# Order of the first transfers of a decoder trunk layer: the second block of x behind the first weights' loads, the stores of the first h behind the copies of its keys

## The chip, the cores and the metric

The kernel runs on one core of one Trainium2 chip. The metric is the device time of one execution in microseconds (us): the median of three runs is 3142.17 us (3137.32 to 3142.69). A core has TensorE (PE, with its weight loads shown apart as PEld), VectorE (DVE), ScalarE (ACT), GpSimd (POOL) and SyncE (SP). Nearly all transfers of this kernel are issued by SP, one after the other, and all of them are carried by the same set of 16 DMA engines.

## The reference, cut to what matters

One decoder layer on a sequence of 2048 tokens with 1024 features, all float32. The conditioning vector c gives shifts, scales and gates; the normed and modulated x goes through one input projection; two kinds of causal attention run on 8 heads each; then come an output projection with a gated residual, a gated MLP with a short convolution, and a last norm.

```python
mod = jax.nn.silu(c) @ w_ada[l] + b_ada[l]
shift_a, scale_a, gate_a, shift_m, scale_m, gate_m = [...]
h = rms_norm(x, g_attn[l]) * (1.0 + scale_a) + shift_a
proj = h @ w_in[l]
q_f, k_f, v_f, q_s, k_s, v_s, f_logit = jnp.split(proj, offsets, axis=-1)
...
o_fox = forgetting_attention(...); o_sb = stick_breaking_attention(...)
x = x + gate_a * (mix @ w_out[l])
h = rms_norm(x, g_mlp[l]) * (1.0 + scale_m) + shift_m
u = causal_depthwise_conv(h @ w_up[l], conv_w[l], conv_b[l])
x = x + gate_m * ((jax.nn.silu(u_gate) * u_val) @ w_down[l])
return rms_norm(x, g_final)
```

## The kernel before, in words

Tokens are worked in four blocks of 512 (`TB`), features in eight tiles of 128 (`kt`). A matrix product in float32 is made of three products of a high and a low part, so that each operand is split: `split` copies the rounded value with ACT (line 44) and subtracts it from the source with DVE or POOL (line 45).

The attention is worked in 32 units (kind, pair of heads, block), first the stick-breaking kind ("sb"). While one unit attends, the projections of the next one are worked in between (`interleave`). The order of the instructions on each engine's queue isn't the order of the program: a planner simulates the kernel's instructions and puts each on its engine's queue when it is ready in that simulation; earlier lines of the program go first among ready ones. The queues themselves are then worked in order, SP's too: a transfer whose operand isn't ready holds up all that stand behind it on SP.

The unit ("sb", 0, 0) stands alone at the start, and it also makes what the others need:

- `load_x` (line 173) brings a block of x as four tiles of 128 tokens. There are four buffers `xt`, so the second block can be loaded as soon as the transposes of the first have read it.
- `mod_cols(kt)` brings two pieces of `w_ada` (line 206; three buffers `ada`, one in use per `kt`) and multiplies them with silu(c): DVE takes five of eight parts (lines 209 and 211), ACT three (line 213) with POOL (line 215), then TensorE sums over the partitions (line 220), and DVE makes the column of shift and scale `mod_a` (lines 221, 222).
- `load` in `load_w` brings a tile of `w_in` (line 256; three buffers `wraw` for the query/key and the value columns together) and splits it. In `prepare` there is one query/key tile for each `kt`, and at the last `kt` also the eight tiles `raw_v` of the values.
- `modulate` norms x (lines 93 to 95 and 104), transposes it (line 112), applies shift and scale (line 117 with ACT for the first block, line 115 with DVE for the others) and splits it to `hp` (lines 44 and 45). There are ten buffers `hp`.
- `done` (line 364) stores each finished `hp` to DRAM (`hs`, line 366), where units of other heads fetch it (line 346), and accumulates the queries and, for the first block, the keys (line 281).
- `finish_proj` splits queries and keys, copies them with SP to the layout of the attention (Q: line 293, K: line 303), projects the values from `hp` (line 320) and stores the values of the next pair of heads (line 337).

The attention of a unit starts with logits (lines 378 and 379), which need Q and K; with line 410 ACT then takes sigmoids, with line 416 DVE scans them.

Of the kernel before, what the change touches and what calls it, by code (L numbers as in the profile page):

```python
# [1 line left out]

# [14 lines left out]
P = 128  # L17
S = 2048
D = 1024
KT = D // P  # L20
HD = 64
NH = 8
NPAIR = 8
TB = 512
# [9 lines left out]
def kernel(ctx: ExitStack, tc: tile.TileContext, x, c, w_ada, b_ada, g_attn, w_in, b_fgate,  # L34
                      g_out_fox, g_out_sb, w_out, g_mlp, w_up, conv_w, conv_b, w_down, g_final, out):
    nc = tc.nc
    x, out = x[0], out[0]
    w_ada, w_in, w_out, w_up, conv_w, w_down = w_ada[0], w_in[0], w_out[0], w_up[0], conv_w[0], w_down[0]

    def f(t):  # L40
        return t.bitcast(F32)
# [8 lines left out]
    hs = [[dram.tile([P, 2, TB], F32, name=f"hs{t}_{k}") for k in range(KT)] for t in range(NTB)]  # L50
# [107 lines left out]
    sb = open_pool("sb", side="right")  # L158
# [8 lines left out]
    pt = lambda: bank(psb, "pt", 3)  # L167
    pv = lambda: bank(psb, "pv", 1)

    def load_x(tb):  # L170
        xts = [px.tile([P, D], F32, name="xt", tag="xt", bufs=4) for _ in range(TB // P)]
        for i, xt in enumerate(xts):
            nc.sync.dma_start(xt, x[tb * TB + i * P:tb * TB + (i + 1) * P, :])
        return xts

    def h_tile():
# [26 lines left out]
    def mod_cols(kt):  # L203
        w = sm.tile([P, KT, 2, P], F32, name="ada", bufs=3)
        for i in range(2):
            nc.sync.dma_start(w[:, :, i], w_ada[:, i * D + kt * P:i * D + (kt + 1) * P].rearrange(
                "(k p) n -> p k n", p=P))
        t = sm.tile([P, 2, P], F32, name="adas", bufs=2)
        nc.vector.tensor_scalar_mul(t, w[:, 0], cs[:, 0:1])
        for k in range(1, 5):  # L210
            nc.vector.scalar_tensor_tensor(t, w[:, k], cs[:, k:k + 1], t, ALU.mult, ALU.add)
        for k in range(5, KT):
            nc.scalar.activation(w[:, k], w[:, k], AF.Copy, scale=cs[:, k:k + 1])
            if k > 5:
                nc.gpsimd.tensor_add(w[:, 5], w[:, 5], w[:, k])
        ts = [t, w[:, 5]]
        b = pv()
        for i in range(2):
            for n, t in enumerate(ts):
                nc.tensor.matmul(b[:, i:i + 1], t[:, i], ones[:, 0:1], start=n == 0, stop=n == len(ts) - 1)  # L220
        nc.vector.tensor_add(mod_a[:, 1, kt:kt + 1], b[:, 0:1], cols[:, R_BA + kt:R_BA + kt + 1])
        nc.vector.scalar_tensor_tensor(mod_a[:, 0, kt:kt + 1], b[:, 1:2], cols[:, R_GA + kt:R_GA + kt + 1],
                                       gba[:, kt:kt + 1], ALU.mult, ALU.add)
# [26 lines left out]
    def load_w(kind, p):  # L250
        base = (0 if kind == "fox" else 3 * 512) + p * P
        lo_engine = nc.vector if kind == "sb" else None

        def load(tag, kt, first, step):
            raw = sl_.tile([P, 2, P], F32, name=f"raw_{tag}", tag="wraw", bufs=3)
            nc.sync.dma_start(raw, w_in[kt * P:(kt + 1) * P, first:first + (step + 1) * P].rearrange(
                "p (a n) -> p a n", n=P)[:, 0:step + 1:step, :])
            n = 2 * P + (NH if tag == "v" else 0)
            w_ = sl_.tile([P, 2, n], F32R, name=f"w_{tag}", bufs=8)
            w = w_[:, :, 0:2 * P].rearrange("p s (a n) -> p s a n", n=P)  # L260
            split(w[:, 0], w[:, 1], raw, lo_engine)
            if tag == "v" and (kind, p) == ("sb", 0):
                split(w_[:, 0, 2 * P:], w_[:, 1, 2 * P:], wfr[:, kt], nc.vector)
            return w if tag == "qk" else w_

        def load_qk(kt):
            qk_.append(load("qk", kt, base, 4))

        def load_v():
            return [load("v", kt, base + 1024, 1) for kt in range(KT)] if p % 2 == 0 else None  # L270

        qk_ = []
        if (kind, p) == ("sb", 0):
            return [qk_, load_qk, load_v]
        for kt in range(KT):
            load_qk(kt)
        return [qk_, load_v()]
# [5 lines left out]
    def finish_proj(kind, p, tb, aq, w, hts, res, ak=None):  # L283
        Q = sb.tile([P, 2, 2, TB], F32R, name="Q", bufs=2)
        K = sb.tile([P, 2, TB], F32R, name="K", bufs=5)
        V = sb.tile([P, 4, 2, P], F32R, name="V", bufs=6)
        q2 = sl_.tile([P, 2, TB], F32R, name="q2", bufs=2)
        k2 = sl_.tile([P, 2, TB], F32R, name="q2", bufs=2)
        nc.scalar.activation(q2[:, 0], aq, AF.Copy, scale=-HD ** -0.5)
        nc.vector.scalar_tensor_tensor(q2[:, 1], aq, -HD ** -0.5, f(q2[:, 0]), ALU.mult, ALU.subtract)  # L290
        for h in range(2):
            for r in range(2):
                nc.sync.dma_start(f(Q[r * HD:(r + 1) * HD, h]), f(q2[h * HD:(h + 1) * HD]))
        if ak is None:
            ak = pj()
            for kt in range(KT):
                accumulate(ak, 1, w[0], hts[kt], kt)
                if kt % 2:
                    yield
        split(k2[:, 0], k2[:, 1], ak, nc.vector)  # L300
        for h in range(2):
            for r in range(2):
                nc.sync.dma_start(f(K[r * HD:(r + 1) * HD, h]), f(k2[h * HD:(h + 1) * HD, r]))
        yield
        spill = vs[kind][p // 2][tb]
        if p % 2:
            nc.sync.dma_start(f(V), spill)
        else:
            V1 = sb.tile([P, 4, 2, P], F32R, name="V", bufs=6)
            forget = (kind, p) == ("sb", 0)  # L310
            step, width = (1, 2 * P + NH) if forget else (2, 2 * P)
            if forget:
                zn = px.tile([P, 4, NH], F32, name="zn", bufs=1)
            for i in range(0, 4, step):
                av = pj()
                for t in range(step):
                    tok = slice((i + t) * P, (i + t + 1) * P)
                    for kt in range(KT):
                        for m, (a, bb) in enumerate(((0, 0), (0, 1), (1, 0))):
                            nc.tensor.matmul(av[:, t * width:(t + 1) * width], hts[kt][:, a, tok],  # L320
                                             w[1][kt][:, bb, 0:width],
                                             start=kt == 0 and m == 0, stop=kt == KT - 1 and m == 2)
                        if kt % 4 == 3:
                            yield
                if forget:
                    nc.vector.tensor_copy(zn[:, i], av[:, 2 * P:width])
                av = av[:, 0:step * 2 * P].rearrange("p (t e h d) -> p t e h d", t=step, e=2, h=2)
                for e, v in enumerate((V, V1)):
                    v = v[:, i:i + step]
                    split(v[:, :, :, 0:HD], v[:, :, :, HD:P], av[:, :, e], nc.vector)  # L330
            if forget:
                b = pt()
                nc.tensor.transpose(b[0:4 * NH, 0:P], zn.rearrange("p t n -> p (t n)"), ident)
                zt = px.tile([4 * NH, P], F32, name="zt", bufs=1)
                nc.scalar.activation(zt, b[0:4 * NH, 0:P], AF.Identity, bias=bf_c)
                nc.sync.dma_start(zs[tb], zt)
            nc.sync.dma_start(spill, f(V1))
        res.append((Q, K, V))
        yield
# [13 lines left out]
    def norm_proj(tb, xts, w, res):  # L353
        aq = pj()
        ak = qk() if tb == 0 else None
        def prepare(kt):
            mod_cols(kt)
            w[1](kt)
            if kt == KT - 1:
                w[1:] = [w[2]()]  # L360

        hts = []

        def done(kt, h):
            hts.append(h)
            nc.sync.dma_start(hs[tb][kt], f(h))
            accumulate(aq, 0, w[0], h, kt)
            if ak is not None:
                accumulate(ak, 1, w[0], h, kt)

        yield from modulate(px, pt, xts, mod_a, lambda kt: h_tile(), done, "a", nc.vector if tb == 0 else None, tb > 0,
                            f(sb.tile([P, 2, 2 * 2 * P], F32R, name="at", bufs=3)).rearrange("p a n -> p (a n)"),
                            prepare if tb == 0 else None)
        yield from finish_proj("sb", 0, tb, aq, w, hts, res, ak)

    def logits(cw, qcols, hl, Q, K):
        b = qk()
# [281 lines left out]
    for i, u in enumerate(units):  # L659
        kind, p, tb = u  # L660
# [13 lines left out]
        if kind == "fox":  # L674
            n = sum(2 * (2 + 2 * tb + j2 + 1) for j2 in range(2)) + 1
        else:
            n = sum(2 * (tb + 1 + 2 * tb + j2 + 1) for j2 in range(2)) + 1
        if i >= len(units) - 2:
            head_scale(i - len(units) + 2, pt(), sx)
        if nxt is None:  # L680
# [4 lines left out]
            loaded = [load_o(0, p) for p in range(3)]  # L685
# [37 lines left out]
    for u in range(NU):  # L723
# [3 lines left out]
        xts = []  # L727
# [293 lines left out]
```

## Time and profile before

| | |
|---|---|
| median of three runs | 3142.17 us (3137.32 to 3142.69) |
| the profiled execution | 3141.04 us, of which the span is 3139.3 us |
| TensorE matmuls | 2967.0 us busy, 95% of the span |
| TensorE weight loads | 2511.6 us, 80% |
| DVE / ACT / POOL | 2145.5 / 1691.0 / 1227.1 us |
| TensorE's granted clock, mean | 0.983 |
| first stretch, 0 to 80 us | PE busy 53.37 us, clock 0.89, DMA at 262 GB/s |

A row of the timeline gives start in us, length in us, engine, line, operation, what is written from what is read, the number of merged instructions, and in brackets the idle time of the engine before it with what ended it. SPq and ACTq are the issuing of transfers by SP and ACT: their length is the time of the issue and not that of the transfer. A row of a table by stages gives start and end, length, then for PE, PEld, DVE, ACT and POOL the busy time with the number of instructions, then the granted clock, the share of the DMA engines and the GB/s moved.

### The profile page before, as it was taken

The numbers are of one execution on the slowest core, as the hardware profiler recorded it, in microseconds if no ns is written. First come the engines' busy times: TensorE is split into PE (matmuls) and PEld (weight loads), VectorE is DVE, ScalarE is ACT, GpSimd is POOL, SyncE is SP. The second block draws the span as 40 slices with busy tenths as digits, with TensorE's granted clock in tenths as the row PEclk, the third lists the DMA queues.
The fourth block names the chain that finished last, engine by engine and source line by source line (L and its number), as shares of the span: only waits on it lengthen the run. The fifth ranks groups of instructions, "written<-read, shape, count | busy, mean of one in ns | idle before, by whom it ended". The sixth has DMA issues, their size and how long they took to land. (4 is left out here: it accounts for less than half of the span.)

```text
span 3139.3 us, 46425 instructions
## 1 busy us (share of the span) xinstructions
PE 2967.0 (95%) x15934; PEld 2511.6 (80%) x15934; DVE 2145.5 (68%) x3342; ACT 1691.0 (54%) x3161; POOL 1227.1 (39%) x1387
## 2 busy tenths in 40 slices
PE   6889998989989999999999999999899998999998
PEld 5778787877878889888877678888678887888887
DVE  6787888878875876556843587778987776354253
ACT  5666776666756676567744444444444444343332
POOL 1554455456553242242212344344444442322321
PEclk8999999999999999999999999999999999999999
DMA  9547542555336696585446632222222223554552
GB/s 267 177 140 255 168 136 69 182 185 155 123 108 221 214 314 211 158 313 162 164 158 222 212 97 86 86 83 83 82 82 89 85 81 130 190 199 161 189 199 90
DMA packets 292940, 496.51 MB, mean 158 GB/s; under 512 B 29448, under 2 KB 177664, under 8 KB 291680
## 3 DMA queue, kind: packets, MB, share of 16 engines
q1 hardware_dynamic: 281072, 480.92, 47.9%
q10 hardware_dynamic: 11632, 12.63, 1.1%
q8 instruction: 126, 2.06, 0.3%
q14 instruction: 110, 0.90, 0.1%
HBM read 352.61 MB, written 90.51 MB: 141 GB/s over the span
## 5 line engine op out<-in xcount | busy, mean ns | idle before, releaser
L810 PE MATMUL ps_o<-oa,wu 128*128 128x512 f32 x2088 | 503.5, 392 | 14.4 <-DVE oa L45 6.9
L810 PEld LDWEIGHTS ps_o<-oa,wu 128*128 128x128 f32 x2088 | 390.5, 188 | 105.5 <-DVE oa L45 10.7
L397 PE MATMUL ps_pv<-at,V 128*128 128x256 f32 x2304 | 410.9, 296 | 41.6 <-DVE at L393 24.8
L393 DVE TENSOR_TENSOR at<-ps_pt,at 128x512 fp32r<-128x512 f32 (+1 forms) x576 | 366.0, 653 | 102.8 <-ACT at L392 99.8
L281 PE MATMUL ps_pj<-hp,w_qk 128*128 128x512 f32 x1512 | 418.4, 406 | 11.1 <-ACT hp L44 3.1
L420 POOL TENSOR_TENSOR a<-a,r 128x512 f32<-128x512 f32 (+3 forms) x240 | 283.4, 1182 | 368.8 <-DVE r L416 112.3
L392 ACT ACTIVATE at<-ps_pt 128x512 fp32r<-128x512 f32 (+1 forms) x576 | 319.4, 577 | 179.8 <-PE ps_pt L388 147.3
L397 PEld LDWEIGHTS ps_pv<-at,V 128*128 128x128 f32 x2304 | 337.0, 192 | 84.6 <-DVE at L393 42.8
L281 PEld LDWEIGHTS ps_pj<-hp,w_qk 128*128 128x128 f32 x1512 | 275.7, 191 | 65.4 <-POOL hp L45 4.0
L45 DVE TENSOR_TENSOR wd<-wdraw,wd 128x1024 fp32r<-128x1024 f32 x88 | 112.4, 1277 | 261.4 <-ACT wd L44 261.4
L378 PE MATMUL ps_qk<-K,Q 128*128 128x512 f32 (+2 forms) x640 | 264.1, 414 | 11.3 <-DMA K<-q 5.8
L419 DVE TENSOR_TENSOR_SCAN r<-r 128x513 f32<-128x513 f32 x192 | 258.0, 1355 | 21.7 <-ACT r L410 14.5
L45 POOL TENSOR_TENSOR g<-graw,g 128x512 fp32r<-128x512 f32 x84 | 141.3, 1684 | 326.8 <-ACT g L44 326.8
L960 PE MATMUL ps_o<-wd,g 128*128 128x512 f32 x1040 | 250.8, 391 | 8.8 <-ACT g L44 8.8
L810 PE MATMUL ps_t<-ob,wu 128*128 128x512 f32 x984 | 243.2, 392 | 0.0
L320 PE MATMUL ps_pj<-w_v,hp 128*128 128x256 f32 (+1 forms) x1536 | 234.1, 291 | 4.8 <-DVE q L45 2.2
L379 PE MATMUL ps_qk<-K,Q 128*128 128x512 f32 (+2 forms) x640 | 238.1, 373 | 0.0
L960 PEld LDWEIGHTS ps_o<-wd,g 128*128 128x128 f32 x1040 | 196.2, 189 | 50.0 <-ACT g L44 9.2
L44 ACT ACTIVATE wu<-wuraw 128x512 fp32r<-128x512 f32 x214 | 133.2, 626 | 185.5 <-PE ps_o L810 111.5
L320 PEld LDWEIGHTS ps_pj<-w_v,hp 128*128 128x128 f32 x1536 | 211.8, 193 | 15.5 <-DVE q L45 3.1
L810 PEld LDWEIGHTS ps_t<-ob,wu 128*128 128x128 f32 x984 | 186.2, 189 | 39.4 <-DVE wu L45 0.3
L388 PE MATMUL ps_pt<-edge,a 128*128 128x128 f32 x1088 | 187.3, 281 | 27.6 <-POOL a L420 14.7
(217 smaller groups left out, 5743.3 us busy)
## 6 DMA issues: line engine op xcount, KB each, us to landing
hp<-hs SPq DMA_DIRECT2D x224, 512.0 KB
wuraw<-in_w_up_dram SPq DMA_DIRECT2D x84, 512.0 KB
wdraw<-in_w_down_dram SPq DMA_DIRECT2D x84, 512.0 KB
Q<-q SPq DMA_DIRECT2D x128, 256.0 KB
g<-u SPq DMA_DIRECT2D x42, 512.0 KB
graw<-g SPq DMA_DIRECT2D x84, 256.0 KB
hs<-hp SPq DMA_DIRECT2D x32, 512.0 KB
K<-q SPq DMA_DIRECT2D x128, 128.0 KB
```

Source lines behind the costliest of these rows:

```text
L45: (lo_engine or nc.gpsimd).tensor_sub(lo, src, f(hi))
L281: nc.tensor.matmul(acc, w[kt][:, a, n], h[:, bb], start=kt == 0 and i == 0, stop=kt == KT - 1 and i == 2)
L320: nc.tensor.matmul(av[:, t * width:(t + 1) * width], hts[kt][:, a, tok], w[1][kt][:, bb, 0:width], start=kt == 0 and m == 0, stop=kt == KT ...
L378: nc.tensor.matmul(b[:, :cw], Q[:, hl, 0, qcols], K[:, hl, :cw], start=True, stop=False)
L379: nc.tensor.matmul(b[:, :cw], Q[:, hl, 1, qcols], K[:, hl, :cw], start=False, stop=True)
L392: nc.scalar.activation(at[:, 0, lo:], b[:, lo:], AF.Copy)
L393: nc.vector.tensor_sub(at[:, 1, lo:], b[:, lo:], f(at[:, 0, lo:]))
L397: nc.tensor.matmul(o[:, 0:2 * P], V[kt // 4][:, kt % 4, hl, :], rhs, start=first and kk == 0 and w == 0, stop=last and kk == 1 and w == 1)
L419: nc.vector.tensor_tensor_scan(rev, rev, rev, 1.0, ALU.mult, ALU.bypass)
L420: (nc.vector if (ch + qi) % 4 == 0 else nc.gpsimd).tensor_mul(a[:, :need], a[:, :need], r[:, 1:need + 1])
L810: nc.tensor.matmul(b, w[:, p, j], o[:, q], start=first and i == 0, stop=last and i == 2, skip_group_check=True)
L960: nc.tensor.matmul(banks[t][n], g[:, a, t * P:(t + 1) * P], w[:, b, n * TB:(n + 1) * TB], start=k == 0 and i == 0, stop=k == NKD - 1 and i ...
```

## The change

Two groups of transfers of the first stretch get an earliest place on SP's queue. `tc.issue_after(ins)` makes every instruction of the block that runs on the engine of `ins` stand behind `ins` on that engine's queue. It gives an order of issue alone: nothing waits for the transfer of `ins` to have landed.

- The list `first_loads` collects the loads of `w_ada` (line 206) and the loads of `w_in` of ("sb", 0) (line 256). The block of x loaded first is loaded while the list is empty and stays as it is. The second block of x (and the later ones) is issued behind the last of them, the load of the eighth tile `raw_v`.
- The stores of the eight `hp` of the first block go from `done` to a place behind the last of the four copies of the first K (line 303). The stores of the later blocks stay in `done`.

The same tiles and the same bytes are moved as before.

```diff
+    first_loads, copied = [], []
+
+    def behind_first_loads():
+        return tc.issue_after(first_loads[-1].ins) if first_loads else nullcontext()
+
     def load_x(tb):
         xts = [px.tile([P, D], F32, name="xt", tag="xt", bufs=4) for _ in range(TB // P)]
-        for i, xt in enumerate(xts):
-            nc.sync.dma_start(xt, x[tb * TB + i * P:tb * TB + (i + 1) * P, :])
+        with behind_first_loads():
+            for i, xt in enumerate(xts):
+                nc.sync.dma_start(xt, x[tb * TB + i * P:tb * TB + (i + 1) * P, :])
         return xts
...
-            nc.sync.dma_start(w[:, :, i], w_ada[...])
+            first_loads.append(nc.sync.dma_start(
+                w[:, :, i], w_ada[...]))
...
+            if (kind, p) == ("sb", 0):
+                first_loads.append(loaded)
...
-                nc.sync.dma_start(f(K[r * HD:(r + 1) * HD, h]), f(k2[h * HD:(h + 1) * HD, r]))
+                copied[:] = [nc.sync.dma_start(f(K[r * HD:(r + 1) * HD, h]), f(k2[h * HD:(h + 1) * HD, r]))]
...
         def done(kt, h):
             hts.append(h)
-            nc.sync.dma_start(hs[tb][kt], f(h))
+            if tb:
+                nc.sync.dma_start(hs[tb][kt], f(h))
...
-        yield from finish_proj("sb", 0, tb, aq, w, hts, res, ak)
+        finish = finish_proj("sb", 0, tb, aq, w, hts, res, ak)
+        if tb == 0:
+            next(finish)
+            with tc.issue_after(copied[-1].ins):
+                for kt, h in enumerate(hts):
+                    nc.sync.dma_start(hs[tb][kt], f(h))
+        yield from finish
```

More of the change, by code (lines that the diff above doesn't have):

```diff
@@ L1 @@
-from contextlib import ExitStack
+from contextlib import ExitStack, nullcontext
 import concourse.bass as bass
@@ L205, in mod_cols @@
         for i in range(2):
-            nc.sync.dma_start(w[:, :, i], w_ada[:, i * D + kt * P:i * D + (kt + 1) * P].rearrange(
-                "(k p) n -> p k n", p=P))
+            first_loads.append(nc.sync.dma_start(
+                w[:, :, i], w_ada[:, i * D + kt * P:i * D + (kt + 1) * P].rearrange("(k p) n -> p k n", p=P)))
         t = sm.tile([P, 2, P], F32, name="adas", bufs=2)
@@ L255, in load @@
             raw = sl_.tile([P, 2, P], F32, name=f"raw_{tag}", tag="wraw", bufs=3)
-            nc.sync.dma_start(raw, w_in[kt * P:(kt + 1) * P, first:first + (step + 1) * P].rearrange(
+            loaded = nc.sync.dma_start(raw, w_in[kt * P:(kt + 1) * P, first:first + (step + 1) * P].rearrange(
                 "p (a n) -> p a n", n=P)[:, 0:step + 1:step, :])
+            if (kind, p) == ("sb", 0):
+                first_loads.append(loaded)
             n = 2 * P + (NH if tag == "v" else 0)
```

## The prediction, made before the result was known

> **What bounds the kernel now.** I read the page first (span, the row of slices, the sizes of the transfers), then tables by stages to see which stretch the change can reach, then the timelines of SP, DVE, ACT and PE over the first 80 us. The chain of waits that ended last doesn't reach back to the start, so the start has to be read from the timelines themselves.
>
> ```profile
> span 3139.3 us, 46425 instructions
> hs<-hp SPq DMA_DIRECT2D x32, 512.0 KB
> xt<-in_x_dram SPq DMA_DIRECT2D x16, 512.0 KB
> ```
>
> ```profile
> 14.60:50.60 36.00, 27.25 (x117) 20.97 (x118) 30.54 (x71) 21.91 (x50) 11.98 (x14) 0.86 1.16 325
> ...
> 60.00:70.00 10.00, 6.39 (x41) 5.48 (x39) 6.50 (x17) 4.59 (x12) 0.00 (x0) 0.95 0.90 210
> 70.00:80.00 10.00, 9.85 (x67) 9.74 (x68) 3.31 (x11) 3.01 (x14) 0.78 (x5) 0.83 0.15 34
> ...
> 80.00:200.00 120.00, 104.61 (x649) 90.61 (x649) 91.72 (x135) 78.07 (x172) 65.56 (x76) 0.94 0.48 164
> 200.00:800.00 600.00, 550.60 (x3484) 479.81 (x3483) 501.37 (x686) 403.94 (x893) 306.94 (x460) 0.98 0.53 165
> 800.00:1560.00 760.00, 730.08 (x4790) 650.58 (x4790) 528.00 (x1223) 504.11 (x980) 278.35 (x368) 0.99 0.62 200
> ```
>
> The reader is to see that from 14.6 to 50.6 us the DMA engines are full (share 1.16, 325 GB/s) and that DVE is close to full as well: 30.54 of 36 us. From 70 to 80 us the same engines are nearly empty (0.15, 34 GB/s), while PE is busy for 9.85 of 10 us. So bytes moved from the first stretch to the second lie beside other work. Which of DMA and DVE holds up the first stretch decides how much is won.
>
> SP's issues of the transfers in question:
>
> ```profile
> 1.20 1.78 SPq L173 DMA_DIRECT2D xt<-in_x_dram  x4
> ...
> 23.77 0.35 SPq L366 DMA_DIRECT2D hs<-hp  x1
> ...
> 29.24 0.42 SPq L366 DMA_DIRECT2D hs<-hp  x1
> ...
> 36.57 1.64 SPq L366 DMA_DIRECT2D hs<-hp  x1
> ...
> 40.15 0.38 SPq L366 DMA_DIRECT2D hs<-hp  x1
> 40.63 1.52 SPq L206 DMA_DIRECT2D ada<-in_w_ada_dram  x2
> 42.24 4.00 SPq L173 DMA_DIRECT2D xt<-in_x_dram  x3
> ...
> 48.24 0.88 SPq L256 DMA_DIRECT2D raw_v<-in_w_in_dram  x2
> ...
> 53.50 5.17 SPq L366 DMA_DIRECT2D hs<-hp  x2
> 59.43 0.84 SPq L256 DMA_DIRECT2D raw_v<-in_w_in_dram  x2
> 61.24 1.18 SPq L303 DMA_DIRECT2D K<-q  x2
> 62.52 3.18 SPq L293 DMA_DIRECT2D Q<-q  x4
> 65.80 2.30 SPq L303 DMA_DIRECT2D K<-q  x2
> 68.20 1.57 SPq L256 DMA_DIRECT2D raw_qk<-in_w_in_dram  x3
> ...
> 195.47 0.38 SPq L256 DMA_DIRECT2D raw_qk<-in_w_in_dram  x1
> ```
>
> Four stores stand ahead of the last pair of w_ada pieces, the second block of x is issued right behind that pair and ahead of five of the eight raw_v, and the last two raw_v leave 1.8 us before the first copy of K.
>
> **The change part by part.**
>
> **Stores of h.** Four of the eight stores stand ahead of the last w_ada pair. Four times 512 KB is 2.10 MB, at 325 GB/s 6.5 us of the DMA engines. That is the most that the pair can land earlier. What DVE can use of it is its own idle time after the first store; these are the rows in which it waited until it began the last `mod_cols`:
>
> ```profile
> 32.43 0.35 DVE L209 TENSOR_SCALAR adas<-ada,cs 128x256 f32<-128x256 f32 x1 [0.83 <-DMA ada<-in_w_ada_dram]
> 33.11 0.69 DVE L45 TENSOR_TENSOR hp<-hf_a,hp 128x512 fp32r<-128x512 f32 x1 [0.33 <-ACT hp L44]
> ...
> 38.75 0.16 DVE L221 TENSOR_TENSOR mod_a<-ps_pv,cols 128x1 f32<-128x1 f32 x1 [0.54 <-PE ps_pv L220]
> ...
> 47.78 0.16 DVE L221 TENSOR_TENSOR mod_a<-ps_pv,cols 128x1 f32<-128x1 f32 x1 [0.19 <-PE ps_pv L220]
> ...
> 49.63 0.69 DVE L45 TENSOR_TENSOR hp<-hf_a,hp 128x512 fp32r<-128x512 f32 x1 [1.49 <-ACT hp L44]
> 50.59 0.35 DVE L209 TENSOR_SCALAR adas<-ada,cs 128x256 f32<-128x256 f32 x1 [0.26 <-DMA ada<-in_w_ada_dram]
> ```
>
> Their sum is 0.83 + 0.33 + 0.54 + 0.19 + 1.49 + 0.26 = 3.6 us. DVE works in order, so its waits for ACT or PE go as well only if the next weights are there to be worked on; with the DMA relieved they are. I take 3.6 us, since DVE is the nearer limit; the bounds are nothing (other waits in the same places) and the 6.5 us of the bytes. On SP eight issues of some 0.4 us leave the first 60 us; SP is idle between issues there, so that counts for nothing by itself.
>
> Behind the copies of K the stores are 4.2 MB, 13 us at 325 GB/s. The cover is the stretch from 62 to 80 us, which moves 34 GB/s at its end. Cost: nothing. If the cover were gone, the ring of ten `hp` would show it: two buffers are free, so the third `hp` of the second block would wait for the first store, by at most the 13 us of all stores. Behind the stores on SP stand the three weight loads of 68.20, whose buffers are asked for again only at 195.47 us, so that nobody waits for them early.
>
> **Second block of x.** It moves from 42.24 us to behind the last raw_v. What leaves its old place, beside 2.10 MB, is its norm: squares on ACT and scalings on DVE that stand between h and the keys now.
>
> ```profile
> 60.01 1.42 DVE L104 TENSOR_SCALAR xt<-xt,ss_a 128x1024 f32<-128x1024 f32 x2
> 61.34 0.68 DVE L290 SCALAR_TENSOR_TENSOR q<-ps_pj,q 128x512 fp32r<-128x512 f32 x1
> 61.95 1.41 DVE L104 TENSOR_SCALAR xt<-xt,ss_a 128x1024 f32<-128x1024 f32 x2
> 63.27 0.68 DVE L45 TENSOR_TENSOR q<-ps_qk,q 128x512 fp32r<-128x512 f32 x1
> ```
>
> ```profile
> 55.94 1.04 ACT L93 ACTIVATE at<-xt 128x1024 f32<-128x1024 f32 x1
> ...
> 56.98 0.62 ACT L44 ACTIVATE hp<-hf_a 128x512 fp32r<-128x512 f32 x1
> ...
> 67.72 1.28 ACT L410 ACT_TABLE_LOAD   x1
> ```
>
> ```profile
> 70.15 0.39 PE L378 MATMUL ps_qk<-K,Q 128*128 128x256 f32 x1 [3.59 <-DMA K<-q]
> ...
> 78.70 0.60 PE L112 MATMUL ps_pt<-edge,xt 128*128 128x128 f32 x4
> ```
>
> The last `hp` stands 1.04 us behind a square: I take 0.9 us of that. The low parts of q and k stand between scalings of 2.83 us; the low part of k can start 2.0 us earlier (the one pair ahead of it costs 1.41, and the first pair pushes q by about 0.6 of its 1.42, as q's high part comes late anyway). K is landed at 70.15 us and PE has waited 3.59 us for it, so a K that comes earlier moves PE at once. I take 2.0 us. Bounds: 0 (if SP's issues of the Q copies, 3.18 us, are the limit anyway) and the 2.83 us of all four scalings. The raw_v are no longer behind x, so the splits of the value weights move forward into DVE's and ACT's waits, at no cost.
>
> The second block is needed at 78.70 us by the transposes. Even with raw_v at their old 59.43 us, the bytes of x take 6.5 us, then four squares of 1.04 us and four scalings of 0.71 follow: 59.4 + 0.8 + 6.5 + 4.2 + 0.7 is about 72 us. It fits by 6 us. If it slipped behind the sigmoids of the first attention, two table loads of 1.28 us would come on top: 2.6 us, the bound of this term upwards.
>
> The unknown of this part is where x stands against K. The trace doesn't show the new place. If raw_v leaves well ahead of K's copies, x is carried before them and costs 0. If it leaves right ahead, all its 2.10 MB are in front, up to 6.5 us. I take 0: the two stores that stand there now (issued at 53.50) go away, and the buffers of raw_v come free earlier without x in front of them.
>
> **The sum.** 3.6 + 0.9 + 2.0 = 6.5 us off. The profiled execution took 3141.04 us: 3134.5 us. It is 1.1 us under the median of the runs, so the forecast for a median is 3135.7 us, about 0.2% less, which is also about what a measurement of this kernel can tell from no change. Since all later work follows from data and not from a fixed time, I carry the shift to the end unshortened.
>
> **The rivals.**
>
> *x collides with the copies of K.* All of x in front of K costs 6.5 us and takes back the whole gain: 3142.2 us. For it: 1.8 us between the last raw_v and K in the rows above, and x ready long before. Against it: raw_v itself moves forward. It decides from the point where raw_v leaves less than 6 us ahead of K. The Trainium skill, DMA: Bandwidth & Descriptors, section Queues, rings and completion order, says that descriptors on one DMA engine are consumed in the order of their ring; by that rule, K's copies can't overtake x issued before them, and the time would be that of this rival. The trace agrees as far as it goes: the w_ada pair behind the four stores was issued at 40.63 and used first at 50.59 us, 10 us later.
>
> *The change frees what wasn't the limit.* DVE is busy for 30.54 of 36 us; if its waits only change places, because the value weights' splits now stand in them ahead of the last h, the 3.6 us stay and only the 2.9 us of the norm go: 3139.3 us. For it: most of these waits name ACT and PE, not the weights (1.09 of 3.6 us).
>
> *Replanning costs more than the start wins.* The planner orders all queues by simulated times; a start that is some us shorter can give another order in the attention, where PE has 120 - 104.61 = 15.4 us of idle time up to 200 us and 600 - 550.60 = 49.4 us up to 800 us, 9% of 720 us together, but only 29.9 us of 760, 4%, in the stretch after. The same planner thus makes orders that differ by five points in idle time, though for different work. Two points more over 720 us are 14.4 us: 3135.7 + 14.4 = 3150.1 us, slower than before. It decides from 13 us, 1.8 points. Against it: the program's order, which breaks ties, stays for all but twelve transfers.
>
> **How the numbers follow.** My forecast has a chance of 0.43, with the gain of a kinder order in it; the collision 0.20, the wait that only moves 0.14, replanning that costs 0.23. Faster by over 0.2% then has 0.45 (the forecast's case, and a little of the others when the order helps), within 0.2% 0.32, slower 0.23. The forecast's own range: all bytes used (6.5 + 0.9 + 2.8 = 10.2 us) gives 3132, x partly in front (+3) gives 3139. The range for 8 in 10: down to 3126, where a better order adds some 6 us (under one point of the idle share) to the full 10.2; up to 3150, where the replanning case stands.
>
> **What would show it right or wrong.** In the profile after, the last w_ada use on DVE (line 209) should begin at about 47 us, not 50.6; no square of x should stand before the last `hp` of the first block, and no scaling before the low part of k; the first logits should begin at about 63.6 us, not 70.15; the transposes of the second block at about 72 us. The stores should run from 60 to 78 us without any engine's wait naming them. Collision: issues of x less than 6 us ahead of K, and PE waiting for K for longer than 3.59 us. Waits that only move: DVE's busy share up to 50 us unchanged. Replanning: the first logits early, but PE's idle time between 80 and 800 us more than 64.8 us by over 13. The prediction is wrong if the order of issue on SP puts raw_v behind K, so that x comes after 70 us and the second block's transposes wait for it.

## The result, and the profile after

The changed kernel is slower: 3147.46 us median of 16 runs (3139.76 to 3153.96) against 3142.08 us of 16 runs of the kernel before (3136.12 to 3148.32). The ratio is 1.0018, with a 95% interval of 1.0009 to 1.0026. The profiled execution took 3149.26 us, its span 3147.5 us.

The start became shorter, as forecast, but by less. These are SP's issues in the profile after (start, length of the issue, what is issued):

```profile
31.06 4.76 SPq L212 DMA_DIRECT2D ada<-in_w_ada_dram  x4
...
38.16 1.58 SPq L212 DMA_DIRECT2D ada<-in_w_ada_dram  x2
39.83 12.30 SPq L262 DMA_DIRECT2D raw_v<-in_w_in_dram  x6
52.22 2.11 SPq L179 DMA_DIRECT2D xt<-in_x_dram  x4
...
60.53 3.20 SPq L301 DMA_DIRECT2D Q<-q  x4
64.25 3.58 SPq L311 DMA_DIRECT2D K<-q  x4
67.87 8.27 SPq L388 DMA_DIRECT2D hs<-hp  x8
```

Both groups stand where the change puts them: x behind the last raw_v, 10 us ahead of K, and the eight stores behind K. What DVE, ACT and PE make of it, in the profile after:

```profile
46.37 0.35 DVE L215 TENSOR_SCALAR adas<-ada,cs 128x256 f32<-128x256 f32 x1 [0.45 <-DMA ada<-in_w_ada_dram]
...
61.19 0.69 DVE L45 TENSOR_TENSOR q<-ps_qk,q 128x512 fp32r<-128x512 f32 x1 [0.69 <-ACT q L44]
```

```profile
53.97 0.62 ACT L44 ACTIVATE hp<-hf_a 128x512 fp32r<-128x512 f32 x1
...
56.88 1.06 ACT L93 ACTIVATE at<-xt 128x1024 f32<-128x1024 f32 x1 [1.31 <-DMA xt<-in_x_dram]
```

```profile
69.37 0.35 PE L393 MATMUL ps_qk<-K,Q 128*128 128x256 f32 x1 [2.67 <-DMA K<-q]
...
74.95 0.60 PE L112 MATMUL ps_pt<-edge,xt 128*128 128x128 f32 x4
...
102.14 6.13 PE L328 MATMUL ps_pj<-w_v,hp 128*128 128x264 f32 x48 [0.72 <-DVE q L298]
111.07 7.48 PE L328 MATMUL ps_pj<-w_v,hp 128*128 128x264 f32 x48 [2.79 <-DVE zn L334]
118.38 0.28 PE L393 MATMUL ps_qk<-K,Q 128*128 128x256 f32 x1
...
120.83 0.50 PE L393 MATMUL ps_qk<-K,Q 128*128 128x512 f32 x1 [1.70 <-ACT a L426]
```

The last pair of w_ada is used from 46.37 and not from 50.59 us, the transposes of the second block begin at 74.95 and not at 78.70 us: 3.75 us earlier. The same stretch of PE's timeline in the profile before shows where this gain goes:

```profile
105.90 6.13 PE L320 MATMUL ps_pj<-w_v,hp 128*128 128x264 f32 x48 [0.72 <-DVE q L290]
114.26 0.39 PE L378 MATMUL ps_qk<-K,Q 128*128 128x256 f32 x1 [2.23 <-DMA K<-q]
...
114.84 4.67 PE L320 MATMUL ps_pj<-w_v,hp 128*128 128x264 f32 x24
119.35 0.40 PE L378 MATMUL ps_qk<-K,Q 128*128 128x512 f32 x1
...
120.28 3.10 PE L320 MATMUL ps_pj<-w_v,hp 128*128 128x264 f32 x24
```

At 102.14 us after, the second unit's value products (the products of `hp` with the value weights) begin, still 3.76 us ahead of 105.90 us. Then the orders part. Before, half of the value products (48) are followed by the first logits of that unit, 24 more products, more logits, and the last 24. After, the planner has put all 96 value products first, and the first logits come at 118.38 us, 4.1 us later than before. PE has waited 2.79 us between the two halves meanwhile, and waits 1.70 us for the sigmoids behind the logits. The store of a unit's output is a mark that all traces have (SP, line 509 before, 524 after). The first and second of them are, before and then after:

```profile
112.74 0.54 SPq L509 DMA_DIRECT2D os<-oT  x1
...
172.65 0.33 SPq L509 DMA_DIRECT2D os<-oT  x1
```

```profile
108.53 0.53 SPq L524 DMA_DIRECT2D os<-oT  x1
...
177.36 0.33 SPq L524 DMA_DIRECT2D os<-oT  x1
```

4.21 us ahead at the first mark, 4.71 us behind at the second. The table by stages says the same of 105 to 180 us, before and then after:

```profile
105.00:180.00 75.00, 65.45 (x435) 58.84 (x433) 53.92 (x86) 49.25 (x110) 33.24 (x41) 0.95 0.48 155
```

```profile
105.00:180.00 75.00, 61.35 (x404) 54.41 (x403) 52.15 (x78) 42.27 (x96) 34.59 (x41) 0.95 0.43 136
```

PE has done 31 matmuls fewer in it, though the second unit's products began earlier, and the DMA engines are less loaded, not more. The two traces' orders of instructions differ in the start, in the attention from the second unit up to about 450 us and in the output projection from 1600 us, and are the same between.

### The profile page after: what moved, and what is told of

Read it like the earlier page. It is cut to its first block, busy times and chain, and to the rows that moved or that the text cites. A ratio compares the mean times of both kernels' runs of the same rounds, so it can differ in the third digit from the quotient of the medians.

```text
span 3147.5 us, 46408 instructions
## 1 busy us (share of the span) xinstructions
PE 2968.0 (94%) x15934; PEld 2517.3 (80%) x15934; DVE 2161.4 (69%) x3342; ACT 1690.3 (54%) x3161; POOL 1249.4 (40%) x1387
```

## The experiments

The theory after this reading: the moves win some 4 us, and the planner's new order costs more than that. The rival: the moved transfers cost something later, whatever the order. To tell them apart, kernels were made in which the moves and the order are chosen apart from one another. The planner is run twice: first for one version, whose order on each engine is kept, then for the version to be run, with edges that hold its instructions to that order. The edges order the issue only and add no wait. Up to the end of the first unit's projection the order is always the version's own.

```diff
+    for moves, (lo, hi) in ORDERS:
+        last = {}
+        for k in plan(moves):
+            if not lo <= k < hi:
+                continue
+            i = by_key[k]
+            if i.engine in last:
+                tc.add_manual_dep(i, last[i.engine].name, NoSync)
+            last[i.engine] = i
```

`MOVES` says which moves the version that runs makes: (x behind the first weights, stores behind the copies of K). An entry of `ORDERS` names a version in the same way and a part of the program, from one mark to another, in which that version's order is held; `plan` gives that order. The marks: "units" is the end of the first unit's projection, "unit2" the end of what is traced for the second unit's attention, "out" the beginning of the output projection, None the end.

**Moves with the old order, and the old places with the new order.**

```diff
-MOVES, ORDERS = (True, True), []
+MOVES, ORDERS = (True, True), [((False, False), ("units", None))]
```

> Both moves of the change, but from the second unit on every engine's queue is held to the order that the planner gave the kernel before. Theory (the planner's new order costs more than the start wins): the 3.75 us that the start wins in the changed kernel's trace stay to the end, so about 3138 us, 0.12% under before. Rival (the moved transfers themselves cost something later, whatever the order): no faster than before, up to 0.18% slower as the changed kernel is.

Measured: 3140.75 us against 3145.29 us of before on the same chip, ratio 0.9986 (0.9978 to 0.9995). Some 4.4 us faster.

```diff
-MOVES, ORDERS = (True, True), []
+MOVES, ORDERS = (False, False), [((True, True), ("units", None))]
```

> All transfers in their old places, but from the second unit on every queue is held to the order that the planner gave the changed kernel. Theory (the order costs): slower than the changed kernel by the start's 3.75 us, so about 3151 us, 0.3% over before. Rival (the moved transfers cost): as before, within 0.1%.

Measured: 3153.99 us, ratio 1.0027 (1.0015 to 1.0039). Some 8.5 us slower, with all transfers where they were.

Together: the moves are worth some 4 us, the order costs 8.5 us by the second kernel and some 10 us by the difference between the changed kernel (1.0018) and the first (0.9986). The rival falls, since the moved transfers cost nothing in the first of the two and aren't there in the second.

**Each move alone, planner free.**

```diff
-MOVES, ORDERS = (True, True), []
+MOVES, ORDERS = (True, False), []
```

> The second block of x behind the first weights, the stores of h in their old places, planner free. Theory: the first logits a little earlier than 70.15 us by the squares and scalings that leave (some 1 to 3 us); the end is what the planner makes of it, anywhere from 5 us under to 10 us over before. Rival: if x is what costs, slower by all of the 0.18%.

Measured: 3143.92 us, ratio 0.9994 (0.9984 to 1.0004).

```diff
-MOVES, ORDERS = (True, True), []
+MOVES, ORDERS = (False, True), []
```

> The stores of the first h behind the copies of K, x in its old place, planner free. Theory: the start wins up to 3.6 us (last use of w_ada at about 47 us); the end is what the planner makes of it, from 5 us under to 10 us over before. Rival: if the stores are what costs, slower by all of the 0.18%.

Measured: 3142.92 us, ratio 0.9998 (0.9987 to 1.0008). Neither move alone can be told from no change, and neither costs the 0.18%. The first logits came at 73.21 us with x alone and at 67.96 us with the stores alone (70.15 before), but the first output left 4.43 us earlier than before in the first case and only 1.63 us earlier in the second. With x alone the first logits are later than before and not, as expected, a little earlier. When they begin is thus no measure of the start, as PE fills the time with value products. The two traces also show which move turns the order. With x alone the second unit keeps the order of the kernel before. With the stores alone three of its four lots of 24 value products stand ahead of its first logits (117.79 us, with the same wait of 2.79 us before the third lot), so that a part of the new order is there already.

**Which order costs: that of the attention or that of the work after it.**

```diff
-MOVES, ORDERS = (True, True), [((False, False), ("units", None))]
+MOVES, ORDERS = (True, True), [((False, False), ("units", "out")), ((True, True), ("out", None))]
```

> Both moves; on every queue the attention units hold the order of the kernel before, and all work from the output projection on holds the order of the changed kernel. Theory now: the order of the attention units between 105 and 180 us costs what the change lost, so about as fast as with the old order everywhere (0.9986 of before). Rival: the order of the output projection costs it (its trace lost 5 us there), so about 5 us slower than with the old order everywhere, 1.000 of before.

Measured: 3139.01 us against 3145.41 us, ratio 0.9977 (0.9968 to 0.9986).

```diff
-MOVES, ORDERS = (True, True), [((False, False), ("units", None))]
+MOVES, ORDERS = (True, True), [((True, True), ("units", "out")), ((False, False), ("out", None))]
```

> The opposite: the attention units hold the order of the changed kernel, all work from the output projection on that of the kernel before. Theory: as slow as the changed kernel, 1.0018 of before. Rival (the output projection's order costs): 5 us less than the changed kernel, about 1.000 of before.

Measured: 3148.55 us, ratio 1.0006 (0.9996 to 1.0016). The two differ by 0.29%, 9 us, and the faster one has the old attention: the order of the attention costs. Taken by itself the second kernel lies nearer to the rival's 1.000 than to the 1.0018 expected, so that it is the pair that decides. The order of the rest shows no cost of one sign: with the old attention the new rest is lower (0.9977 against 0.9986), with the new attention it is higher (1.0018 against 1.0006), and the intervals overlap both times. A cost of the new rest of up to some 4 us beside the new attention (1.0018 less 1.0006) isn't ruled out by this.

**Each move alone with the old order.**

```diff
-MOVES, ORDERS = (True, True), [((False, False), ("units", None))]
+MOVES, ORDERS = (True, False), [((False, False), ("units", None))]
```

> The second block of x behind the first weights alone, the stores in their old places, the old order held from the second unit on. If the two parts of the start add up to the 4.4 us of both moves, the sum of this one and of the stores alone is 4.4 us; by the squares and scalings that leave, this one is worth 1 to 3 us. By the trace of x alone with a free planner, in which the first logits came at 73.21 and not 70.15 us, it may also be worth nothing.

Measured: 3142.95 us, ratio 0.9992 (0.9983 to 1.0001).

```diff
-MOVES, ORDERS = (True, True), [((False, False), ("units", None))]
+MOVES, ORDERS = (False, True), [((False, False), ("units", None))]
```

> The stores of the first h behind the copies of K alone, x in its old place, the old order held from the second unit on. By the trace of the stores alone with a free planner (first logits at 67.96 and not 70.15 us) worth about 2 us; if the stores carry the whole gain, 4 us.

Measured: 3147.03 us, ratio 1.0007 (0.9998 to 1.0016). Neither is clear of no change, and the stores alone miss the 2 to 4 us that were expected of them: the interval leaves at most 0.02%. Alone they don't add up to the 0.14% of both, but the intervals are too wide to say that they help one another; how the gain divides stays open. In the traces the first output leaves at 110.81 and 111.11 us with the stores alone and at 108.31 and 112.50 us with x alone (112.74 before).

**Which place in the attention.** The trace points to the second unit's logits behind its value products.

```diff
-MOVES, ORDERS = (True, True), [((False, False), ("units", None))]
+MOVES, ORDERS = (True, True), [((False, False), ("units", "unit2")), ((True, True), ("unit2", None))]
```

> Both moves; what is traced for the second unit's attention and the third unit's projection holds the order of the kernel before, all later work the order of the changed kernel. Theory (the second unit's stretch carries the loss): 0.998 to 0.9985 of before. Rival (the later units carry it): 1.001.

Measured: 3137.03 us (6 runs) against 3145.45 us, ratio 0.9967 (0.9955 to 0.9978), faster than either side expected.

```diff
-MOVES, ORDERS = (True, True), [((False, False), ("units", None))]
+MOVES, ORDERS = (True, True), [((True, True), ("units", "unit2")), ((False, False), ("unit2", None))]
```

> The opposite: only the second unit's attention with the third unit's projection holds the order of the changed kernel, all later work that of the kernel before. Theory: 1.001 to 1.002 of before. Rival: 0.998 to 0.9985.

Measured: 3149.77 us, ratio 1.0017 (1.0008 to 1.0027). The new order in this one stretch costs all that the changed kernel lost, and the old order in this one stretch, with the changed kernel's order in all the rest, gives the fastest of all versions. PE's timeline from 102 us on, first with the old order in the stretch, then with the new one:

```profile
102.66 6.12 PE L337 MATMUL ps_pj<-w_v,hp 128*128 128x264 f32 x48 [0.72 <-DVE q L307]
110.63 0.54 PE L402 MATMUL ps_qk<-K,Q 128*128 128x256 f32 x1 [1.84 <-DMA K<-q]
...
111.60 4.28 PE L337 MATMUL ps_pj<-w_v,hp 128*128 128x264 f32 x24
```

```profile
101.67 6.13 PE L337 MATMUL ps_pj<-w_v,hp 128*128 128x264 f32 x48 [0.72 <-DVE q L307]
110.59 8.82 PE L337 MATMUL ps_pj<-w_v,hp 128*128 128x264 f32 x48 [2.79 <-DVE zn L343]
119.25 0.28 PE L402 MATMUL ps_qk<-K,Q 128*128 128x256 f32 x1
```

PE's longest waits from 102 to 180 us (in all, how many, the longest), again first with the old order, then with the new one:

```profile
PE ps_qk L402 <- ACT a L435: 2.0, 1, 2.0
PE ps_pv L421 <- DVE oT L531: 1.9, 1, 1.9
PE ps_qk L402 <- DMA K<-q: 1.8, 1, 1.8
```

```profile
PE ps_pj L337 <- DVE zn L343: 2.8, 1, 2.8
PE ps_pj L298 <- POOL hp L46: 2.7, 1, 2.7
PE ps_qk L402 <- ACT a L435: 1.9, 2, 1.7
```

The second store of an output left at 168.09 us in the first and at 178.41 us in the second:

```profile
168.09 0.33 SPq L533 DMA_DIRECT2D os<-oT  x1
```

```profile
178.41 0.33 SPq L533 DMA_DIRECT2D os<-oT  x1
```

Ten microseconds for one choice of order, with the same transfers at the start. With the old order PE's wait for K is 1.84 us and the attention begins 8.6 us earlier; the value products fill PE while ACT and DVE make the first weights. With the new order PE is given all value products at once, must wait until DVE has copied products of the first half out (2.79 us), and has nothing left to do while the sigmoids run (1.7 us). The wait of 2.0 us for a sigmoid in the first list comes at 175.06 us and belongs to the third unit, which has the changed kernel's order there.

All traces on record agree on this. From the first to the second store of an output it took 58.9 to 61.5 us in the nine that have the old order in the second unit, whether the transfers were moved or not, and 68.4 to 70.1 us in the four that have the new one; the stores alone, with a part of the new order, took 62.8.

**The same without holding whole queues.** The changed kernel with a free planner, and one rule more:

```diff
+                            if (kind, p, tb) == ("sb", 0, 1) and i >= 2:
+                                late_v[i].append(mm.ins)
...
+        if attending == [("sb", 0, 1)] and len(first_logits) < 4:
+            first_logits.append(mm.ins)
+            group = late_v.get({2: 2, 4: 3}.get(len(first_logits)), ())
+            for ins in group:
+                tc.add_manual_dep(ins, mm.ins.name, NoSync)
```

> The changed kernel with a free planner and one more rule of order: on TensorE's queue the value products of the third and fourth 128 tokens of the second unit stand behind that unit's first and second pairs of logits. Theory: this one choice costs what the start wins and more, and the later queues follow from it, so with it put right the whole is as fast as with the old order of the attention, 0.998 of before. Rival (the loss comes from the later units' orders by themselves): no better than the changed kernel, 1.0018.

Measured: 3141.12 us against 3145.45 us, ratio 0.9982 (0.9972 to 0.9991). The planner then gave the whole attention the order of the kernel before but for a few instructions next to the rule. So the later differences in the attention followed from this one choice, and most of those in the output projection too: there as well the order is nearly that of the kernel before.

**The kernel before against itself.**

```diff
     pv = lambda: bank(psb, "pv", 1)
+
+
```

> The kernel before itself with blank lines in its source and nothing else changed, to see how far one and the same program differs from itself: a ratio within 0.1% of 1, and in the trace the same places of the attention within 1 us; how far the output projection's stretch differs by itself is what the look is for (some 3 to 4 us if what all traces lose there is the execution and not the order).

Measured: 3146.40 us, ratio 1.0002 (0.9992 to 1.0013). Two marks in its trace, the last store of the attention and the first of the MLP, and the same two of the first profile:

```profile
1601.88 0.34 SPq L524 DMA_DIRECT2D os<-oT  x1
...
1842.31 0.34 SPq L916 DMA_DIRECT2D g<-u  x1
```

```profile
1602.06 0.34 SPq L509 DMA_DIRECT2D os<-oT  x1
...
1838.46 0.34 SPq L901 DMA_DIRECT2D g<-u  x1
```

The stretch of the output projection took 240.4 us here and 236.4 us there, in one and the same program. So the 5 us that the changed kernel's trace lost between these marks aren't shown to be its own. My bound of 1 us for the attention's marks was too narrow as well: the second store was 1.44 us and the fifth 3.43 us off.

## Why the prediction was wrong, step by step

**Stores of h off the start: right in direction; that the number fits is luck.** I took 3.6 us, DVE's idle time, and the last use of w_ada begins 4.2 us earlier (46.37 against 50.59). But the idle time isn't what went. From the first use of w_ada to the last, DVE was idle for 36.00 - 30.54 = 5.5 us before, and after for 32.14 - 27.83 = 4.3 us:

```profile
14.23:46.37 32.14, 26.77 (x104) 22.54 (x104) 27.83 (x64) 19.56 (x44) 12.30 (x14) 1.00 1.09 268
```

The DMA engines are full as before (share 1.09), though four stores fewer are in this stretch. The last pair of w_ada was issued at 38.16 us and first used 8.2 us later; before, behind the four stores, it was 10 us. Most of the 4.2 us, 2.7 of them, is work that DVE now does behind this point: it begins the last `mod_cols` before the seventh column of `mod_a` (49.28 us), which it made first before (47.78). The rows further on show what is left, before and then after:

```profile
54.88 0.16 DVE L221 TENSOR_TENSOR mod_a<-ps_pv,cols 128x1 f32<-128x1 f32 x1 [1.15 <-PE ps_pv L220]
55.27 0.78 ACT L117 ACTIVATE hf_a<-ps_pt,mod_a 128x512 f32<-128x512 f32 x1 [0.67 <-DVE mod_a L222]
57.65 0.80 PE L281 MATMUL ps_pj<-hp,w_qk 128*128 128x512 f32 x1 [2.81 <-ACT hp L44]
59.52 1.05 PE L281 MATMUL ps_qk<-hp,w_qk 128*128 128x512 f32 x2
```

```profile
52.51 0.16 DVE L227 TENSOR_TENSOR mod_a<-ps_pv,cols 128x1 f32<-128x1 f32 x1 [0.72 <-PE ps_pv L226]
52.88 0.78 ACT L117 ACTIVATE hf_a<-ps_pt,mod_a 128x512 f32<-128x512 f32 x1 [0.22 <-DVE mod_a L228]
58.84 0.62 PE L289 MATMUL ps_qk<-hp,w_qk 128*128 128x512 f32 x2
59.53 1.05 ACT L93 ACTIVATE at<-xt 128x1024 f32<-128x1024 f32 x1
```

The last column of `mod_a` is made 2.4 us earlier (52.51 against 54.88): this is what is left for the term, with x moved as well: two thirds of the 3.6.

**ACT's square away: right, 0.6 of 0.9 us.** No square stands before the last h (the first one begins at 56.88 us, the copy of the last h at 53.97). From ACT's modulation of the last h (line 117) to that copy it took 56.98 - 55.27 = 1.7 us before and takes 53.97 - 52.88 = 1.1 us after, since splits of value weights stand there now. I had named these splits as costing nothing. At the last h 3.0 us are won in all, of 3.6 + 0.9.

**Scalings away from q and k: right on DVE, but the gain doesn't reach K.** The low part of k starts at 61.19 and not 63.27 us, 2.1 us earlier. Three things stand on the way from the last h to K that I hadn't counted. PE, which waited 2.81 us for the last h before, has value products between the products of queries and keys now; the last product of the keys ends at 58.84 + 0.62 = 59.46 us against 60.57, only 1.1 us earlier. On ACT a square of the second block (59.53 us) stands between the copies of q and of k. On SP the copies of Q go ahead of all four of K, so that K's first copy is issued at 64.25 us, though k's low part was done at 61.88, and K's last issue ends at 64.25 + 3.58 = 67.83 us against 68.10 us: of the bounds I gave, the lower one held, nothing. The first logits came 0.8 us earlier, not 6.5. PE used the time for value products, so that the transposes came 3.75 us earlier.

**The sum of the start.** 6.5 us were forecast; 3.75 us are in the trace, and some 4.4 come out of the kernel with the old order. The other traces say the same: the transposes of the second block begin at 74.45 to 75.89 us in the seven with both moves and at 77.84 to 80.04 us in the three with neither, and the first output leaves at 108.28 to 109.69 us against 111.70 to 113.84. So the size is about two thirds, and the way is another one than I wrote: not through an earlier K, but through value products that PE does while it would wait.

**Stores behind K, x in time, no collision: right.** x is issued from 52.22 to 54.33 us, 10 us ahead of K, so that the Trainium skill's rule on the order of a ring (DMA: Bandwidth & Descriptors, Queues, rings and completion order) wasn't put to the test here. The same passage of the Trainium skill also says that a later descriptor may finish its write before an earlier one, so that my "can't overtake" goes further than it does. The 10 us from the issue of the w_ada pair to its use, which I took for agreement, aren't the stores' doing alone: without them it was 8.2 us. The last store is issued by 67.87 + 8.27 = 76.14 us, in the stretch that was nearly empty before (34 GB/s) and is full now:

```profile
70.00:80.00 10.00, 10.00 (x67) 9.38 (x66) 6.78 (x15) 6.55 (x22) 2.71 (x8) 0.84 1.02 406
```

No wait of PE in the second unit names the stores. One of DVE does, 1.25 us ahead of 101.40 us; the same instruction waits for 1.25 us before as well, put down to ACT there, so that the stores cost nothing at this place.

**"I carry the shift to the end unshortened": the step that failed.** That holds only for the same order, as the first two experiments show. With the planner free, the new order of the second unit cost some 10 us by the runs (1.0017 with it and 0.9986 without it, with both moves and the old order in all the rest), and some 9 us between the first two outputs in the traces. This is the third rival, in kind and in sign, to which I gave 0.23; I sized it as 14 us spread over 720, and it was one choice in one unit. My reason against it, that the program's order breaks ties, doesn't protect: the value products come first in the program, and taking them first is just what cost. The kernel became slower where I had forecast a gain; that the time still lies within my range is owed to this rival alone, whose 3150 us were its upper end.

## What to carry to other kernels

Where a planner orders the queues, a shift of the start by a few microseconds is also a new order of everything behind it; before a small gain is judged, the old order should be held behind the change and the change measured with that. If the free version loses, the first place where the two traces stop being shifted copies of one another is the place to look at: here it was the choice that costs, and one rule of order there was enough. Work that can fill an engine's waits (here the value products) was best kept behind the work that others wait for (here the logits).

## What was not expected

One program's profiles differ by several microseconds in one stretch: the output projection of the kernel before took 236.4 us in one execution and 240.4 in another, with a mean granted clock of 0.97 and 0.96 from 1602 to 1850 us. A single profile therefore can't place a loss of 4 us there.

The fastest version, with the old order in the second unit's stretch alone, took 0.9967 (0.9955 to 0.9978) of before, faster than with the old order everywhere (0.9986, 0.9978 to 0.9995). The intervals just touch, and the faster one has 6 runs only; that the changed kernel's later orders are better by themselves is possible and not shown. Why the planner's simulation turned to the other choice in the second unit also stays open; the stores alone already turn a part of it, x alone doesn't.
